# Moving 20 modulation dots from the first feed-forward into both attentions, with a new order of its work and ten wide block pairs

## The chip, the cores and the metric

The kernel runs on one core of a Trainium2 chip. The metric is the device time of one execution in microseconds (us). TensorE (PE in the profile, with PEld for its weight loads) does the matrix products, VectorE (DVE), ScalarE (ACT) and GpSimd (POOL) the elementwise work. SyncE (SP) computes nothing: its queue issues most of the transfers from DRAM, one behind the other, and an issue that has to wait holds up the issues behind it. POOL's queue issues the accumulating transfers.

## The reference

Two layers work on 512 tokens of width 1024. Layer 0 mixes the tokens by stick-breaking attention, layer 1 by an indexer-selected sparse attention (16 heads, a top-k selection, a relative bias). Behind each comes a gated feed-forward of width 2816 with a causal convolution over 3 tokens. All norms and residuals are modulated by six vectors a layer that come from the condition `c`:

```python
cond = silu(c)
for i in range(2):
    mod = cond @ ada_w[i] + ada_b[i]
    sh1, sc1, g1, sh2, sc2, g2 = split(mod, 6)
    h = rms_norm(x, norm_mix[i]) * (1 + sc1) + sh1
    mix = stick_breaking_attention(h, ...) if i == 0 else dsa_attention(h, ...)
    x = x + g1 * mix
    h = rms_norm(x, norm_ffn[i]) * (1 + sc2) + sh2
    x = x + g2 * conv_ffn(h, ...)

def conv_ffn(h, w_up, conv_w, conv_b, w_down):
    u = h @ w_up
    y = conv_b + sum(up[:, j:j + S] * conv_w[j] for j in range(3))   # up: u padded by 2 tokens
    gate, val = split(y, 2)
    return (silu(gate) * val) @ w_down
```

## The kernel before

The transposed activations stand on the partitions by feature, 128 at a time. Every product in full precision is made of three products of a shorter format: high by high, low by high and high by low part. So each weight chunk of 128x1024 (512 KB) is loaded as `raw`, ScalarE copies its high part (`whi`), and the low part (`wlo`) is either a subtraction on VectorE or POOL, or ScalarE's negated copy to which a transfer issued by POOL adds the weight once more from DRAM.

**Modulation dots.** `mod` isn't made by TensorE. `ada_dot` multiplies a loaded chunk of `ada_w` (128x1024) by `cond` on VectorE and sums each row; 48 such dots make one layer's modulation. `DOTS` lists those of layer 1 in order of use: six groups `g` of eight. Some are made early, in attention 0 (`ada_steps` once per head), those of `FFN_DOTS[0]` in the first feed-forward, those of `LATE_DOTS` in the late attention of layer 1, and the last eight in the second feed-forward. In the feed-forwards the chunk is a tile named `ada`, elsewhere a `raw`.

**The feed-forward** is not written out in order. `ffn_plan` lists jobs with their engine, duration, predecessors and rings of buffers; `Plan.order` gives each a latest time, counted back from TensorE's fixed order, and sorts every engine's queue by it. Tables steer it: `LEADS` (how early loads are due), `DOT_SPAN` (over which times the dots are spread), `DOWNS_7` and `ORDER_7` (where TensorE's down products go among the up products), and `DOWN_DMA`, `X_DMA`, `ACT_DMA`, `COMBO_DMA`, `PLAIN_DMA` (which low parts and additions go by ScalarE and an accumulating transfer in place of VectorE). There are 22 blocks `j` of the up weights. From block 7 on `up_7` makes a block by seven products of 256 columns instead of eight, with sums and differences of weights and of activations. Each product is 4 chunks deep. In an unmerged block the weight's high part meets the high and the low activations in two 256-wide matmuls; in a block of `MERGED` one 512-wide matmul does both, the halves land beside each other in the bank, and VectorE adds the second half (`side`, six times a block).

**The late attention** of layer 1 (about 724 to 840 us) goes over 16 heads `h`. One round finishes head h and makes the logits of head n = h+1: for each of four query tiles the products `z` (L1925 to L1927), a masked maximum `nm` on VectorE (L1937), an exponential on ScalarE (L2224), transposes `tr` on TensorE (L2234), copies `pT`. `sums(h)` takes the reciprocal of the row sums (L2336). For every odd head it also sends the reciprocals of a pair of heads through DRAM: `rvd` (L2276) writes them and two `bs` (L2282) read them back spread over partitions, all on SP's queue. `th` are the bias rows of a later head (`load_bias`, L1916). `fill` slips in pieces of the query and output projections; their weights are the other `raw` loads (L613).

Of the kernel before, what the change touches and what calls it, by code (L numbers as in the profile page):

```python
# [19 lines left out]
S = 512  # L20
# [42 lines left out]
DOWNS_7 = [[(7, 1), (8, 1), (9, 2), (10, 2), (11, 2), (12, 1), (13, 1), (14, 2), (15, 1), (16, 2), (17, 1), (18, 1), (19, 2),
            (20, 2), (21, 3)],
           [(6, 2), (7, 1), (8, 1), (9, 1), (10, 1), (11, 2), (12, 1), (13, 2), (14, 1), (15, 1), (16, 1), (17, 2), (18, 2),
            (19, 1), (20, 2), (21, 3)]]
ORDER_7 = [['a1', 'd1', 'a2', 'e', 'd2', 'c1', 'down', 'low', 'c2', 'rest'],
           ['a1', 'd1', 'a2', 'e', 'd2', 'down', 'c1', 'low', 'c2', 'rest']]
WEIGHT_7 = {'a1': 0, 'd2': 0, 'a2': 1, 'd1': 13, 'c1': 13, 'e': 24, 'c2': 24}
TAG_7 = {'a': 'mm', 'b': 'x', 'd': 'tr'}  # L70
BANK_7 = {'a1': 'a', 'e': 'a', 'c1': 'a', 'c2': 'a', 'a2': 'b', 'd1': 'd', 'd2': 'd'}
LATE_CHUNKS = [(2, 3), ()]
A_RING = 10
DOT_SPAN = [(30, 310), (5, 270)]
PLAIN_DMA = [[(4, 0), (4, 1), (6, 0), (6, 1)], [(4, 0), (4, 1), (6, 0)]]
DOWN_DMA = [[7, 10, 13, 17, 21], [3, 4, 6, 7, 10, 12, 13, 15, 17, 20, 22]]
LEADS = [{'plain': 38.0, 'r': 8.0, 'sum': 0.5, 'down': 2.0, 'T': 29.5, 'last': 27.5, 'bias': 2.0},
         {'plain': 72.5, 'r': 9.5, 'sum': 3.5, 'down': 3.5, 'T': 10.0, 'last': 0.5, 'bias': 23.0}]
# [160 lines left out]
def ffn_plan(l):  # L239
# [29 lines left out]
    def accumulate(fn, *args, us, after):  # L269
        return p.add("DMA", us * 1.11, None, after=[p.add("POOL", 0.87, fn, *args, after=after)], lag=4.0)  # L270
# [87 lines left out]
    def up_7(j, downs, before):  # L358
        t = p.t
        got1, r1 = load("load_up", j, 1, key=t - lead["r"])  # L360
        got0, r0 = load("load_up", j, 0, key=t - lead["r"] + 0.01)
        s13 = p.add("DVE", 1.22, "sum13", j, after=[got0, got1])
        raw13 = p.place("raw", s13, t - lead["sum"])
        W = {}
        *W[0], n0 = split_by_dma("hi_up", "neg_up", "add_up", (j, 0), r0, got0, 1.05, 3.0, t)
        hi1 = p.add("ACT", 0.62, "hi_half", j, after=[got1])
        both = p.place("whi", hi1, t + 0.1)
        n1 = p.add("ACT", 0.62, "neg_half", j, after=[hi1])
        W[1] = hi1, accumulate("add_half", j, us=1.5, after=[n1]), both, both
# [12 lines left out]
        def then(name, engine, us, fn, arg, needs, ring=None, side=None):  # L382
            if name in done or not all(n in done for n in needs):
                return
            done[name] = p.add(engine, us, fn, j, arg, after=[done[n] for n in needs])
            if ring and ring[0] not in place:
                place[ring[0]] = p.place(ring[1], done[name])
            if merged:
                done[name + "s"] = p.add("DVE", 0.42, "side", j, *side, after=[done[name]])

        def product(what):
            need = [done[n + s_] for n in {"e": ["g0"], "d2": ["v"], "c1": ["x"], "c2": ["v1"]}.get(what, [])]
            if what in ("d1", "d2", "e", "c1"):
# [12 lines left out]
            then("v", "ACT", 0.38, "copy", "v", ["d1"], ("small", "sqt"), ("v", "d"))  # L406
            then("x", "ACT", 0.38, "copy", "x", ["e", "v"], None, ("x", "a"))
            then("v0", "DVE", 0.42, "val", 0, ["x" + s_, "d2"], ("val", "u"), ("v0", "d"))
            then("v1", "DVE", 0.42, "val", 1, ["v" + s_, "c1", "v0"], None, ("v1", "a"))
            then("g2", "ACT", 0.38, "gate", 2, ["c2"], None, ("h", "a"))  # L410

        def finish():
            product("c2")
            place["small"].users += [done["v1"], done["v0"]]
            place["bank a"].users.append(done["g2" + s_])
            place["bank b"].users.append(done["g1" + s_])
            place["bank d"].users.append(done["v0" + s_])
# [24 lines left out]
        return finish  # L442
# [131 lines left out]
def kernel_body(ctx, tc, xT, wst, cst, smalls, crow, ccol, relb, outT):  # L574
# [36 lines left out]
    def chunk_raw(key, n=D):  # L611
        raw = raws.tile([P, D], F32, name="raw")
        nc.sync.dma_start(raw[:, :n], wst[CH[key], :, :n])  # L613
        return raw
# [337 lines left out]
    def stick_layer(l):  # L952
        with ExitStack() as st:
# [481 lines left out]
            for i in range(HN):  # L1435
# [41 lines left out]
    def ffn_layer(l, first, man):  # L1477
        with ExitStack() as st:
# [45 lines left out]
            class do:  # L1524
# [289 lines left out]
    def dsa_layer(l, first, man):  # L1814
        with ExitStack() as st:
# [306 lines left out]
            with ExitStack() as sa:  # L2122
# [218 lines left out]
                for h in range(HEADS):  # L2341
# [210 lines left out]
```

## Time and profile before

| what | us |
|---|---|
| three runs | 1212.32, 1212.98, 1215.43 |
| median | 1212.98 |
| the profiled execution | 1212.47 |
| its span in the trace | 1210.7 |
| TensorE busy | 1204.2 |
| VectorE busy | 1024.2 |
| ScalarE busy | 800.0 |
| POOL busy | 243.5 |

The stages in the trace: attention 0 from about 60 to 262 us, the first feed-forward from about 280 to 603, layer 1's attention from 605 to 862, the second feed-forward to the end. In the rows, `x12` counts instructions, the figure behind it is time, and a bracket such as `[1.66 <-PE tr L2234]` gives the idle time of the engine before the instruction and what ended it. Busy shares are averages over stages; which engine waits for which is read in the stage.

### The profile page before, as it was taken

The numbers are of one execution on the slowest core, as the hardware profiler recorded it, in microseconds if no ns is written. First come the engines' busy times: TensorE is split into PE (matmuls) and PEld (weight loads), VectorE is DVE, ScalarE is ACT, GpSimd is POOL, SyncE is SP. The second block draws the span as 40 slices with busy tenths as digits, with TensorE's granted clock in tenths as the row PEclk, the third lists the DMA queues.
The fourth block names the chain that finished last, engine by engine and source line by source line (L and its number), as shares of the span: only waits on it lengthen the run. The fifth ranks groups of instructions, "written<-read, shape, count | busy, mean of one in ns | idle before, by whom it ended". The sixth has DMA issues, their size and how long they took to land.

```text
span 1210.7 us, 18277 instructions
## 1 busy us (share of the span) xinstructions
PE 1204.2 (99%) x6532; PEld 1009.1 (83%) x6532; DVE 1024.2 (85%) x1736; ACT 800.0 (66%) x1366; POOL 243.5 (20%) x282
## 2 busy tenths in 40 slices
PE   9999999999999999999999999999999999999998
PEld 6888788788898998998888777777888888888887
DVE  5898888998989988999788995668989898889883
ACT  5588787368666676765657357774786677677660
POOL 0001100001111111211000357784012122112110
PEclk9999999999999999999999999999999999999999
DMA  9778897629789898896520242245499888788662
GB/s 377 249 205 231 224 244 240 209 87 220 192 217 277 230 245 217 225 290 174 183 70 18 70 140 57 84 137 167 137 234 212 225 190 204 182 184 190 155 147 87
DMA packets 79923, 224.89 MB, mean 186 GB/s; under 512 B 16588, under 2 KB 17356, under 8 KB 79832
## 3 DMA queue, kind: packets, MB, share of 16 engines
q1 hardware_dynamic: 59616, 169.16, 42.3%
q0 software_dynamic: 20192, 54.54, 25.5%
q8 instruction: 51, 0.84, 0.3%
q14 instruction: 40, 0.33, 0.1%
q10 hardware_dynamic: 24, 0.02, 0.0%
HBM read 212.62 MB, written 2.16 MB: 177 GB/s over the span
## 4 chain that ended last, share of the span: by engine, by line
PE 98%; DMA 1%; ACT 0%; DVE 0%; issue 0%; SPq 0%
PE pt_d L1741 16%; PE pt_a L1653 8%; PE pt_u L1622 6%; PE pt_a L1649 6%; PE pt_d L1653 4%; PE pt_u L1626 3%; PE pt_d L1649 3%; PE pt_q L694 2%; PE pt_q L696 2%; PE pt_l L694 2%; PE pt_q L695 2%; PE pt_l L695 2%; PE pt_l L696 2%; PE pt_qk L694 2%; PE pt_qk L696 2%; PE pt_qk L695 2%
## 5 line engine op out<-in xcount | busy, mean ns | idle before, releaser
L1741 PE MATMUL pt_d<-actlo,dnhi 128*128 128x512 f32 x288 | 112.8, 392 | 0.0
L1741 PE MATMUL pt_d<-acthi,dnhi 128*128 128x512 f32 x288 | 112.8, 392 | 0.0
L1531 ACT ACTIVATE whi<-raw 128x1024 fp32r<-128x1024 f32 x72 | 75.8, 1054 | 29.6 <-PE pt_a L1653 13.1
L644 ACT ACTIVATE whi<-raw 128x1024 fp32r<-128x1024 f32 x80 | 84.2, 1052 | 3.6 <-issue 1.1
L1622 PE MATMUL pt_u<-hh,whi 128*128 128x512 f32 x320 | 75.8, 389 | 0.0
L1741 PE MATMUL pt_d<-acthi,dnlo 128*128 128x512 f32 x288 | 73.5, 391 | 0.0
L662 POOL DMA_DIRECT2D wlo<-wst x23 | 19.9, 866 | 265.2 <-DVE hh L806 114.1
L1622 PEld LDWEIGHTS pt_u<-hh,whi 128*128 128x128 f32 x320 | 60.0, 188 | 12.6 <-issue 0.2
L1543 POOL DMA_DIRECT2D wlo<-wst x37 | 32.0, 865 | 167.1 <-ACT wlo L1539 91.4
L1741 PEld LDWEIGHTS pt_d<-actlo,dnhi 128*128 128x128 f32 x288 | 54.3, 188 | 10.1
L1741 PEld LDWEIGHTS pt_d<-acthi,dnhi 128*128 128x128 f32 x288 | 54.2, 188 | 10.1
L1741 PEld LDWEIGHTS pt_d<-acthi,dnlo 128*128 128x128 f32 x288 | 53.1, 188 | 10.3
L653 POOL TENSOR_TENSOR wlo<-raw,whi 128x1024 fp32r<-128x1024 f32 x18 | 44.2, 2456 | 85.7 <-PE pt_q L695 45.8
L1649 PE MATMUL pt_a<-hh,whi 128*128 128x512 f32 x228 | 61.3, 391 | 0.0
L1349 DVE TENSOR_TENSOR_SCAN mz<-mz,diag 128x768 f32<-128x768 f32 (+1 forms) x32 | 47.6, 1487 | 15.2 <-ACT mz L1343 15.0
L722 DVE SCALAR_TENSOR_TENSOR raw<-raw,cond 128x1024 f32<-128x1024 f32 x46 | 57.3, 1273 | 1.4 <-ACT cond L1167 1.3
L1653 PE MATMUL pt_a<-hh,wlo 128*128 128x256 f32 x360 | 57.4, 282 | 0.0
L1653 PEld LDWEIGHTS pt_a<-hh,wlo 128*128 128x128 f32 x360 | 53.1, 190 | 4.5
L1937 DVE CUSTOM_DVE_ANT_0 L<-z,L,cols 128x128 f32<-128x128 f32 (+3 forms) x60 | 32.3, 546 | 28.7 <-PE tr L2234 20.7
L1554 POOL DMA_DIRECT2D whi<-wst x30 | 26.0, 866 | 132.8 <-ACT whi L1551 82.6
L694 PE MATMUL pt_q<-hh,whi 128*128 128x512 f32 x128 | 51.8, 405 | 0.0
L722 DVE SCALAR_TENSOR_TENSOR ada<-ada,cond 128x1024 f32<-128x1024 f32 x41 | 50.0, 1219 | 1.7 <-DMA ada<-wst 1.7
(409 smaller groups left out, 3803.3 us busy)
## 6 DMA issues: line engine op xcount, KB each, us to landing
raw<-wst SPq DMA_DIRECT2D x215, 512.0 KB, 5.2
wlo<-wst POOLq DMA_DIRECT2D x60, 512.0 KB, 7.8
ada<-wst SPq DMA_DIRECT2D x45, 512.0 KB, 5.4
raw<-wst SPq DMA_DIRECT2D x48, 384.0 KB, 4.8
whi<-wst POOLq DMA_DIRECT2D x30, 256.0 KB, 5.8
dnlo<-wst POOLq DMA_DIRECT2D x16, 384.0 KB, 7.0
x<-xt POOLq DMA_DIRECT2D x18, 256.0 KB, 5.6
th<-relb SPq DMA_DIRECT2D x16, 256.0 KB, 4.0
```

What stands on the lines that cost most here:

```text
L644: act.activation(hi[:, :n], raw[:, :n], AF.Copy)
L653: engine.tensor_sub(lo[:, :w], raw[:, :w], hi[:, :w].bitcast(F32))
L694: pe.matmul(out, lhsT=whi, rhs=ahi, start=start, stop=False)
L695: pe.matmul(out, lhsT=wlo, rhs=ahi, start=False, stop=False)
L696: pe.matmul(out, lhsT=whi, rhs=alo, start=False, stop=stop)
L722: dve.scalar_tensor_tensor(raw, raw, 1.0, cond, op0=OP.mult, op1=OP.mult, accum_out=dst)
L1349: dve.tensor_tensor_scan(rev, rev, diag[:, b:e][:, ::-1], 0.0, OP.mult, OP.max)
L1531: act.activation(W[j, i][0], R[j, i], AF.Copy)
L1622: pe.matmul(pt[j, i], lhsT=W[j, i][0][:, k * P:(k + 1) * P], rhs=hs[k][n], start=k + n == 0, stop=False)
L1649: pe.matmul(pt[j, bank, "both"], lhsT=w[:, c0 + k * P:c0 + (k + 1) * P], rhs=a[2], start=new and k == 0, stop=False, skip_group_check=True)
L1653: pe.matmul(out, lhsT=w[:, c0 + k * P:c0 + (k + 1) * P], rhs=a[n], start=new and k + n == 0, stop=part == 1 and k == 3 and what in ("a2", ...
L1741: pe.matmul(pt["dn", i], lhsT=dn[i][part][:, k * P:(k + 1) * P], rhs=A[j0 + k][n], start=part + k + n == 0, stop=part == 1 and k == j1 - j ...
```

## The change

Of layer 1's dots, 11 instead of 4 are made early in attention 0, 13 instead of 33 in the first feed-forward, and 16 instead of 3 in the late attention, where now each head has one dot behind its reciprocal and each round one load. In the first feed-forward 10 blocks instead of 5 are merged, and the tables move low parts between the engines: for 12 blocks the up weight's low part and for 6 the half weight's go from ScalarE and a transfer to VectorE, and 11 low parts of down weights, 5 additions to `x` and 4 low parts of activations go from VectorE to ScalarE and a transfer. The due times are set anew. The second feed-forward's tables stay as they were.

```diff
-ORDER_7 = [['a1', 'd1', 'a2', 'e', 'd2', 'c1', 'down', 'low', 'c2', 'rest'],
+ORDER_7 = [['a1', 'd1', 'a2', 'e', 'd2', 'c1', 'down', 'c2', 'low', 'rest'], ...
-DOT_SPAN = [(30, 310), (5, 270)]
+DOT_SPAN = [(145, 405), (5, 270)]
-DOWN_DMA = [[7, 10, 13, 17, 21], [3, 4, 6, 7, 10, 12, 13, 15, 17, 20, 22]]
+DOWN_DMA = [[0, 1, 2, 4, 5, 7, 9, 10, 12, 13, 15, 16, 17, 18, 19, 21], [3, 4, 6, 7, 10, 12, 13, 15, 17, 20, 22]]
-MERGED = [[10, 15, 16, 20, 21], [7, 9, 10, 11, 12, 13, 14, 15, 16, 17, 18, 19, 20, 21]]
+MERGED = [[8, 9, 11, 13, 14, 15, 16, 19, 20, 21], [7, 9, 10, 11, 12, 13, 14, 15, 16, 17, 18, 19, 20, 21]]
-X_DMA = [[1, 2, 8, 10, 11, 13, 19, 20, 22, 23], [1, 2, 6, 9, 13, 20, 22, 23]]
-ACT_DMA = [[2, 5, 9, 15], [4, 7, 8, 9, 13, 15, 20]]
+X_DMA = [[0, 2, 5, 6, 9, 10, 12, 14, 15, 16, 18, 19, 20, 21, 23], [1, 2, 6, 9, 13, 20, 22, 23]]
+ACT_DMA = [[3, 4, 5, 6, 7, 12, 14, 19], [4, 7, 8, 9, 13, 15, 20]]
+W0_DVE = [[7, 8, 9, 10, 12, 13, 15, 17, 18, 19, 20, 21], []]
+W1_DVE = [[7, 9, 10, 14, 20, 21], []]
 DOTS = [(1, g, f) for g in range(6) for f in range(8)]
-LATE_DOTS = DOTS[37:40]
-FFN_DOTS = [DOTS[4:37], DOTS[40:]]
+EARLY_DOTS = 11
+LATE_DOTS = DOTS[24:40]
+FFN_DOTS = [DOTS[EARLY_DOTS:24], DOTS[40:]]
...
-        *W[0], n0 = split_by_dma("hi_up", "neg_up", "add_up", (j, 0), r0, got0, 1.05, 3.0, t)
+        if j in W0_DVE[l]:
+            W[0] = split("hi_up", "lo_up", (j, 0), r0, got0, 1.05, 1.22, t)
+            n0 = W[0][1]
+        else:
+            *W[0], n0 = split_by_dma("hi_up", "neg_up", "add_up", (j, 0), r0, got0, 1.05, 3.0, t)
...
+        if j in W1_DVE[l]:
+            n1 = p.add("DVE", 0.69, "lo_half", j, after=[hi1])
+            W[1] = hi1, n1, both, both
+        else:
...
-    ada_jobs = [(0, g, f) for g in (2, 3, 4, 5) for f in range(KT)] + DOTS[:4]
+    ada_jobs = [(0, g, f) for g in (2, 3, 4, 5) for f in range(KT)] + DOTS[:EARLY_DOTS]
...
-                ada_steps(3 if i % 4 == 3 else 2)
+                ada_steps(2 if i % 3 == 2 else 3)
...
+                def lo_half(j):
+                    put((j, 1), 1, W[j, 1][0])
+                    dve.tensor_sub(W[j, 1][1][:, S:], R[j, 1][:, S:], W[j, 1][0][:, :S].bitcast(F32))
...
-                raw_dots = []
+                raw_dots, dots_left = [], list(LATE_DOTS)

                 def load_dots(n):
-                    raw_dots.extend((d, chunk_raw(("ada",) + d)) for d in LATE_DOTS[len(raw_dots):][:n])
+                    for _ in range(min(n, len(dots_left))):
+                        d = dots_left.pop(0)
+                        raw_dots.append((d, chunk_raw(("ada",) + d)))
...
                 load_bias(3)
+                load_dots(1)
...
                     follow(dve)
                     if h == 3:
                         q_newton(8, EARLY_Q)
-                    if h == HEADS - 2:
-                        late_dots(2)
-                    if not more:
-                        late_dots(1)
+                    late_dots(1)
...
                         for j in range(2, QT):
                             masked_bias(h + 2, j)
+                    load_dots(1)
                     if n + 3 < HEADS:
                         load_bias(n + 3)
...
                     if h == HEADS - 4:
-                        load_dots(3)
                         bias_job(2, "col")
```

Three places in the order of instructions. First, TensorE in block 8 of the first feed-forward, which is newly merged: `pt_a`, `pt_d` and `pt_b` are the banks, `hh` activations, `tt` their combinations. Before:

```order
L1653 MATMUL pt_a<-hh,whi 128x256 x8
L1653 MATMUL pt_a<-hh,wlo 128x256 x4
L1653 MATMUL pt_d<-tt,whi 128x256 x8
L1653 MATMUL pt_d<-tt,wlo 128x256 x4
L1653 MATMUL pt_b<-hh,whi 128x256 x12
```

After:

```order
L1663 MATMUL pt_a<-hh,whi 128x512 x4
L1667 MATMUL pt_a<-hh,wlo 128x256 x4
L1663 MATMUL pt_d<-tt,whi 128x512 x4
L1667 MATMUL pt_d<-tt,wlo 128x256 x4
L1663 MATMUL pt_b<-hh,whi 128x512 x4
L1667 MATMUL pt_b<-hh,whi 128x256 x4
```

Eight narrow matmuls have become four wide ones in each product. Lines are those of the changed kernel, where the wide product stands at L1663 and the narrow one at L1667.

Second, SP's queue in the late attention from the `rvd` of heads 6 and 7 to that of heads 8 and 9; numbers are those of buffers. Before:

```order
L2276 DMA rvd_7951<-rv_7762 128x2x4
L2282 DMA bs_7971<-rvd_7951 64x512 x2
L1916 DMA th_8000<-relb 128x512
L1916 DMA th_8084<-relb 128x512
L613 DMA raw_8094<-wst 128x1024
L2276 DMA rvd_8130<-rv_7928 128x2x4
```

After:

```order
L2292 DMA rvd_7836<-rv_7641 128x2x4
L2298 DMA bs_7858<-rvd_7836 64x512 x2
L623 DMA raw_7887<-wst 128x1024
L1930 DMA th_7889<-relb 128x512
L623 DMA raw_7974<-wst 128x1024
L1930 DMA th_7976<-relb 128x512
L623 DMA raw_7986<-wst 128x1024
L2292 DMA rvd_8022<-rv_7813 128x2x4
```

The load `raw_7887` of head 8's dot stands behind the two `bs` of head 7, `raw_7974` of head 9's behind the next `th`.

Third, VectorE at head 8, from its reciprocal `rv` to the maximum of the next head's fourth tile. Before:

```order
L2336 RECIPROCAL rv_7928<-sum_7930 128x4
L1937 ISA L2_7994,nm_8015<-z_8053,L2_7994,cols_6316 128x384
L1937 ISA nm_8015 128x1
L2241 COPY pT_8041<-tr_8059 128x512
L1937 ISA L3_7997,nm_8015<-z_8068,L3_7997,cols_6316 128x512
```

After:

```order
L2353 RECIPROCAL rv_7813<-sum_7815 128x4
L732 SCALAR_TENSOR_TENSOR raw_7887,mod1_88<-raw_7887,cond_86 128x1024
L1951 ISA L2_7881,nm_7904<-z_7943,L2_7881,cols_6178 128x384
L1951 ISA nm_7904 128x1
L2257 COPY pT_7930<-tr_7949 128x512
L1951 ISA L3_7884,nm_7904<-z_7958,L3_7884,cols_6178 128x512
```

The dot of `raw_7887` now stands between the reciprocal and the maximum.

More of the change, by code (lines that the diff above doesn't have):

```diff
@@ L62 @@
 FIRST_7 = [7, 7]
[L63 to L66, printed above, removed]
-ORDER_7 = [['a1', 'd1', 'a2', 'e', 'd2', 'c1', 'down', 'low', 'c2', 'rest'],
-           ['a1', 'd1', 'a2', 'e', 'd2', 'down', 'c1', 'low', 'c2', 'rest']]
+DOWNS_7 = [[(7, 2), (8, 1), (9, 2), (10, 1), (11, 2), (12, 2), (13, 2), (14, 1), (15, 1), (16, 1), (17, 1), (18, 2),
+           (19, 1), (20, 2), (21, 3)], [(6, 2), (7, 1), (8, 1), (9, 1), (10, 1), (11, 2), (12, 1), (13, 2), (14, 1),
+           (15, 1), (16, 1), (17, 2), (18, 2), (19, 1), (20, 2), (21, 3)]]
+ORDER_7 = [['a1', 'd1', 'a2', 'e', 'd2', 'c1', 'down', 'c2', 'low', 'rest'], ['a1', 'd1', 'a2', 'e', 'd2', 'down',
+           'c1', 'low', 'c2', 'rest']]
 WEIGHT_7 = {'a1': 0, 'd2': 0, 'a2': 1, 'd1': 13, 'c1': 13, 'e': 24, 'c2': 24}
@@ L73 @@
 A_RING = 10
-DOT_SPAN = [(30, 310), (5, 270)]
-PLAIN_DMA = [[(4, 0), (4, 1), (6, 0), (6, 1)], [(4, 0), (4, 1), (6, 0)]]
-DOWN_DMA = [[7, 10, 13, 17, 21], [3, 4, 6, 7, 10, 12, 13, 15, 17, 20, 22]]
-LEADS = [{'plain': 38.0, 'r': 8.0, 'sum': 0.5, 'down': 2.0, 'T': 29.5, 'last': 27.5, 'bias': 2.0},
-         {'plain': 72.5, 'r': 9.5, 'sum': 3.5, 'down': 3.5, 'T': 10.0, 'last': 0.5, 'bias': 23.0}]
-FFN_BIAS = [(1, 4), (1, 10)]
-MERGED = [[10, 15, 16, 20, 21], [7, 9, 10, 11, 12, 13, 14, 15, 16, 17, 18, 19, 20, 21]]
-X_DMA = [[1, 2, 8, 10, 11, 13, 19, 20, 22, 23], [1, 2, 6, 9, 13, 20, 22, 23]]
-ACT_DMA = [[2, 5, 9, 15], [4, 7, 8, 9, 13, 15, 20]]
+DOT_SPAN = [(145, 405), (5, 270)]
+PLAIN_DMA = [[(4, 0), (5, 0), (5, 1), (6, 1)], [(4, 0), (4, 1), (6, 0)]]
+DOWN_DMA = [[0, 1, 2, 4, 5, 7, 9, 10, 12, 13, 15, 16, 17, 18, 19, 21], [3, 4, 6, 7, 10, 12, 13, 15, 17, 20, 22]]
+LEADS = [{'plain': 81.5, 'r': 17.0, 'sum': 10.5, 'down': 19.5, 'T': 32.0, 'last': 1.0, 'bias': 131.0}, {'plain': 72.5,
+         'r': 9.5, 'sum': 3.5, 'down': 3.5, 'T': 10.0, 'last': 0.5, 'bias': 23.0}]
+FFN_BIAS = [(1, 0), (1, 6)]
+MERGED = [[8, 9, 11, 13, 14, 15, 16, 19, 20, 21], [7, 9, 10, 11, 12, 13, 14, 15, 16, 17, 18, 19, 20, 21]]
+X_DMA = [[0, 2, 5, 6, 9, 10, 12, 14, 15, 16, 18, 19, 20, 21, 23], [1, 2, 6, 9, 13, 20, 22, 23]]
+ACT_DMA = [[3, 4, 5, 6, 7, 12, 14, 19], [4, 7, 8, 9, 13, 15, 20]]
 XT = 2
-COMBO_DMA = [[(2, 0)], [(1, 0), (1, 1), (3, 0), (3, 1)]]
+W0_DVE = [[7, 8, 9, 10, 12, 13, 15, 17, 18, 19, 20, 21], []]
+W1_DVE = [[7, 9, 10, 14, 20, 21], []]
+COMBO_DMA = [[(2, 1)], [(1, 0), (1, 1), (3, 0), (3, 1)]]
 DOTS = [(1, g, f) for g in range(6) for f in range(8)]
-LATE_DOTS = DOTS[37:40]
-FFN_DOTS = [DOTS[4:37], DOTS[40:]]
+EARLY_DOTS = 11
+LATE_DOTS = DOTS[24:40]
+FFN_DOTS = [DOTS[EARLY_DOTS:24], DOTS[40:]]
 class Job:
@@ L364, in up_7 @@
         W = {}
-        *W[0], n0 = split_by_dma("hi_up", "neg_up", "add_up", (j, 0), r0, got0, 1.05, 3.0, t)
+        if j in W0_DVE[l]:
[3 more added lines that the diff above has]
+            *W[0], n0 = split_by_dma("hi_up", "neg_up", "add_up", (j, 0), r0, got0, 1.05, 3.0, t)
         hi1 = p.add("ACT", 0.62, "hi_half", j, after=[got1])
         both = p.place("whi", hi1, t + 0.1)
-        n1 = p.add("ACT", 0.62, "neg_half", j, after=[hi1])
-        W[1] = hi1, accumulate("add_half", j, us=1.5, after=[n1]), both, both
+        if j in W1_DVE[l]:
+            n1 = p.add("DVE", 0.69, "lo_half", j, after=[hi1])
+            W[1] = hi1, n1, both, both
+        else:
+            n1 = p.add("ACT", 0.62, "neg_half", j, after=[hi1])
+            W[1] = hi1, accumulate("add_half", j, us=1.5, after=[n1]), both, both
         r1.users += [hi1, n1]
```

## Prediction

> **What bounds the kernel now.** I read the page first, then busy time by stage, then the critical chain inside the first feed-forward, then single engines around the three places that the change edits. The page's head, its row of busy times and its chain:
>
> ```profile
> span 1210.7 us, 18277 instructions
> ...
> PE 1204.2 (99%) x6532; PEld 1009.1 (83%) x6532; DVE 1024.2 (85%) x1736; ACT 800.0 (66%) x1366; POOL 243.5 (20%) x282
> ...
> PE 98%; DMA 1%; ACT 0%; DVE 0%; issue 0%; SPq 0%
> ```
>
> TensorE is busy in 1204.2 of 1210.7 us and the chain that ends last is 98% TensorE. So time can only fall if matmuls are removed or made shorter, or if some of the 1210.7 - 1204.2 = 6.5 us without a matmul vanish; it rises when another engine's wait reaches TensorE. The stages that the change edits are attention 0 (60 to 240 us), the first feed-forward (290 to 600) and the late attention of layer 1 (724 to 830):
>
> ```profile
> core 0: us, PE busy (x) PEld busy (x) DVE busy (x) ACT busy (x) POOL busy (x), PEclk, DMA share, GB/s
> 60.00:240.00 180.00, 179.95 (x1036) 145.51 (x1036) 157.20 (x199) 133.21 (x267) 12.93 (x15) 1.00 0.78 224
> 290.00:600.00 310.00, 310.00 (x1826) 275.89 (x1825) 278.30 (x434) 204.20 (x308) 46.78 (x54) 1.00 0.84 226
> 724.00:830.00 106.00, 104.81 (x653) 83.36 (x652) 69.97 (x200) 76.59 (x197) 82.61 (x92) 1.00 0.35 101
> ```
>
> In the feed-forward TensorE never idles, so taking dots off VectorE there relieves nothing that TensorE waits for: the gain is not in the moved dots but at most in what else changes in TensorE's own work. VectorE looks free in the late attention (69.97 of 106 us), but that is an average; what counts is where its idle stretches lie and when a dot's data arrive.
>
> **Merging, the one edit that shortens TensorE's work.** Five more blocks (5 to 10) feed a weight's high part through one 512-wide matmul in place of two 256-wide ones. One product, unmerged and merged, in the critical chain (start, us, what):
>
> ```profile
> 335.18 1.44 PE pt_d L1653 x12
> ...
> 381.77 0.93 PE pt_d L1649 x4
> 382.70 0.47 PE pt_d L1653 x4
> ```
>
> Twelve narrow matmuls take 1.44; four wide and four narrow take 0.93 + 0.47 = 1.40. That is 0.04 us a product, with 7 products in each of 5 blocks: 35 x 0.04 = 1.4 us saved, on the path. The figures are rounded to 0.01 each, so 0.03 to 0.05, or 1.0 to 1.8 us.
>
> **VectorE and the rest in the first feed-forward.** VectorE's groups there (line, engine, operation, shapes, count | busy, mean ns | idle before):
>
> ```profile
> L722 DVE SCALAR_TENSOR_TENSOR ada<-ada,cond 128x1024 f32<-128x1024 f32 x33 | 40.2, 1220 | 1.4 <-DMA ada<-wst 1.4
> L1535 DVE TENSOR_TENSOR wlo<-raw,whi 128x1024 fp32r<-128x1024 f32 x17 | 20.8, 1224 | 5.1 <-ACT whi L1531 4.9
> ...
> L1725 DVE TENSOR_TENSOR dnlo<-raw,dnhi 128x768 fp32r<-128x768 f32 x19 | 18.1, 954 | 1.8 <-ACT dnhi L1722 1.8
> ...
> L1708 DVE TENSOR_TENSOR actlo<-y,acthi 128x512 fp32r<-128x512 f32 x16 | 11.0, 686 | 0.8 <-ACT acthi L1705 0.7
> L816 DVE SCALAR_TENSOR_TENSOR x<-pt_d,mod,x 128x512 f32<-128x512 f32 x14 | 10.5, 748 | 1.5 <-PE pt_d L1741 1.5
> L1566 DVE TENSOR_TENSOR raw<-raw 128x512 f32<-128x512 f32 x15 | 10.3, 688 | 0.2
> ...
> L1689 DVE TENSOR_TENSOR gate<-gate,pt_a 128x256 f32<-128x256 f32 x10 | 4.1, 417 | 0.4 <-ACT gate L1675 0.3
> ```
>
> Away: 20 dots x 1.220 = 24.4; 11 low parts of the down weights x 0.954 = 10.5; 5 additions to x x 0.748 = 3.7; 4 low parts of the activations x 0.686 = 2.7. Added: 5 blocks x 6 side additions x 0.417 = 12.5; 12 low parts of up weights x 1.224 = 14.7 (before, ScalarE and a POOL-issued transfer made them); 6 half-width low parts, of the size of L1566, x 0.688 = 4.1. Net -24.4 - 10.5 - 3.7 - 2.7 + 12.5 + 14.7 + 4.1 = -10.0 us of the 278.3. ScalarE loses 18 negations and gains 20 smaller passes, and with 204.2 of 310 us busy has room. The DMA loses 20 loads of 512 KB, 12 accumulating transfers of 512 KB and 6 of 256 KB, and gains 11 of 384 KB and 9 of 256 KB, under a share of 0.84. I take 0: VectorE, still about 268 of 310 us, and the lighter DMA queues are the cover. Were that cover gone, a late low part would hold TensorE for up to its own length, 1.22 us, and I leave 0 to +2 us for one or two such places among the reshuffled due times. The swap of the low down product and the last product c2 only trades two pieces of TensorE work.
>
> **Attention 0.** Seven more dots, 7 x 1.22 = 8.5 us, in VectorE's idle time of 180 - 157.2 = 22.8 us. Tightest is the last head, where the multiply that makes `a` precedes the transposes on TensorE:
>
> ```profile
> 227.41 0.69 DVE L1350 TENSOR_TENSOR a<-a,mz 128x511 f32<-128x511 f32 x1
> ...
> 229.40 0.60 PE L1366 MATMUL tr<-cons,a 128*128 128x128 f32 x4
> ```
>
> 229.40 - 228.10 = 1.3 us of slack. Steps 12 and 13 take one dot more each, 2.44 us, of which the idle time ahead of this multiply absorbs part; what passes on must exceed 1.3 us to be felt. I take 0, with 0 to +1.
>
> **The late attention: 13 more dots, one behind every reciprocal.** Here the place on two queues decides. On SP the load of the dot for an even head h+1 now stands behind `rvd` and the two `bs` of the odd head h, and `bs` reads what `rvd` wrote to DRAM. On VectorE the dot stands directly behind the head's reciprocal, ahead of the masked max of that head's third tile (L1937, 128x384), which feeds the exponentials and the transposes. Before, the three loads went out at head 12 for dots at heads 14 and 15. SP's rows (start, length) and the transfer time of a 512 KB raw load in this stretch:
>
> ```profile
> 734.91 1.15 SPq L2282 DMA_DIRECT2D bs<-rvd  x2
> 764.41 1.09 SPq L2282 DMA_DIRECT2D bs<-rvd  x2
> 775.19 0.91 SPq L2276 DMA_DIRECT2D rvd<-rv  x1
> 778.92 1.09 SPq L2282 DMA_DIRECT2D bs<-rvd  x2
> 793.71 1.83 SPq L2282 DMA_DIRECT2D bs<-rvd  x2
> 808.70 1.09 SPq L2282 DMA_DIRECT2D bs<-rvd  x2
> ...
> L613 SPq DMA_DIRECT2D raw<-wst x15: 327/426/1239, 753.7 to 844.1; - x15
> ...
> DMA to landing us min/median/max: 3.6/4.9/5.9
> ```
>
> SP's queue stands still from 776.10 (775.19 + 0.91) to 778.92 for that round trip. A load issued at the end of the `bs` pair lands 4.9 us later and its dot ends 1.22 after that, 6.12 us in all. The maxes that would follow:
>
> ```profile
> 741.37 0.62 DVE L1937 CUSTOM_DVE_ANT_0 L<-z,L,cols 128x384 f32<-128x384 f32 x1 [4.23 <-PE tr L2234]
> 770.84 0.62 DVE L1937 CUSTOM_DVE_ANT_0 L<-z,L,cols 128x384 f32<-128x384 f32 x1 [3.60 <-PE tr L2234]
> 783.82 0.62 DVE L1937 CUSTOM_DVE_ANT_0 L<-z,L,cols 128x384 f32<-128x384 f32 x1 [1.66 <-PE tr L2234]
> 798.44 0.62 DVE L1937 CUSTOM_DVE_ANT_0 L<-z,L,cols 128x384 f32<-128x384 f32 x1 [0.30 <-PE tr L2234]
> 812.73 0.62 DVE L1937 CUSTOM_DVE_ANT_0 L<-z,L,cols 128x384 f32<-128x384 f32 x1 [1.37 <-PE tr L2234]
> ```
>
> Lateness of the max: head 2, 736.06 + 6.12 - 741.37 = 0.8; head 6, 765.50 + 6.12 - 770.84 = 0.8; head 8, 780.01 + 6.12 - 783.82 = 2.3; head 10, 795.54 + 6.12 - 798.44 = 3.2; head 12, 809.79 + 6.12 - 812.73 = 3.2. What of it TensorE feels depends on the slack of its next consumers:
>
> ```profile
> 785.75 0.72 ACT L2224 ACTIVATE L<-L,nm 128x512 f32<-128x512 f32 x1 [0.57 <-DVE nm L1937]
> 787.45 0.60 PE L2234 MATMUL tr<-cons,L 128*128 128x128 f32 x4
> ...
> 801.05 0.39 PE L1925 MATMUL z<-kph,qh 128*128 128x256 f32 x1 [0.42 <-DVE nm L1937]
> ...
> 814.66 0.72 ACT L2224 ACTIVATE L<-L,nm 128x512 f32<-128x512 f32 x1 [0.57 <-DVE nm L1937]
> 815.85 0.60 PE L2234 MATMUL tr<-cons,L 128*128 128x128 f32 x4
> ```
>
> Near head 8 the exponential ends at 786.47, 0.98 ahead of the transposes: 2.3 - 0.98 = 1.3 us of stall. Near head 10 TensorE already waits 0.42 for VectorE, so all 3.2 are felt. Near head 12 the exponential ends at 815.38, 0.47 ahead: 3.2 - 0.47 = 2.7. Heads 2 and 6 lie between nothing and all of 0.8; I take half each, 0.8 together. The dots of odd heads are loaded a whole head before their use, with no `rvd` between: 0, at most 1.5 together if their 1.22 us meet a busy VectorE. Sum 1.3 + 3.2 + 2.7 + 0.8 = 8.0 us. With the shortest landing, 3.6, each lateness falls by 1.3 and 0 + 1.9 + 1.4 = 3.3 is left; with the longest, 5.9, it is 2.3 + 4.2 + 3.7 + 2 x 1.8 = 13.8, and 15.3 with the odd heads. I take the median, since these are the same loads in the same stretch.
>
> **The sum.** The profiled execution took 1212.47 us, its span 1210.7 and 1.8 around it, and is 0.5 below the median of the runs. 1212.47 - 1.4 + 0 + 0 + 8.0 = 1219.1 us; with the bounds of the late attention 1214.4 to 1226.4.
>
> **Rivals.** (B) The dots cost nothing there, and only the merging shows: 1212.47 - 1.4 = 1211.1 us, not slower. For it: VectorE idles 1.66 to 4.23 us ahead of several of these maxes, so data that came in time would fit. It decides if a load lands within some 2.5 us of its issue, or if it can leave ahead of the `bs` pair; against it, the shortest landing is 3.6 and the order has it behind. (C) A lock between VectorE and POOL adds to the stalls. The two late dots that ran back to back before:
>
> ```profile
> L722 DVE SCALAR_TENSOR_TENSOR raw<-raw,cond 128x1024 f32<-128x1024 f32 x2 | 4.8, 2440 | 0.0
> ...
> 825.37 3.40 DVE L722 SCALAR_TENSOR_TENSOR raw<-raw,cond 128x1024 f32<-128x1024 f32 x1
> ```
>
> They took 2440 ns on the mean against 1220 elsewhere, and POOL is busy 82.61 of 106 us here with 92 operations, 0.90 us each. A dot that comes at a random moment then waits 0.78 x 0.45 = 0.35 us, 13 x 0.35 = 4.6 in all: 1219.1 + 4.6 = 1223.7. At the rate of those two dots it would be 13 x 1.22 = 15.9; against that, they ran beside a whole weight subtraction on POOL, which most heads don't place there. The Trainium skill ("SBUF — State Buffer", section "Who interferes with whom") says that a VectorE instruction with two SBUF inputs contends with a GpSimd instruction that reads SBUF, and that whoever is first keeps the shared pair for the whole instruction. The 2440 ns agree with it; by that rule the waits would also run the other way, POOL behind a dot. (D) The reordered feed-forward, or the last heads of attention 0, stalls TensorE by its upper ends (+2 and +1) and more, with the late attention free: 1211.1 + 3 = 1214.1 and up; TensorE's 310.00 of 310.00 busy before speaks against it. (E) Faster: the merging's 1.8 and over 2 of the 6.5 us without a matmul vanish together; 1208.8 or less. Nothing in the edits removes a wait that the rows show.
>
> **How the numbers follow.** A measurement of this kernel tells about 0.3%, 3.6 us, from no change. Chances: the forecast 0.60 (0.04 of it within 3.6 us, at the shortest landings), B 0.27, C 0.06, D 0.04 (slower than 0.3%), E 0.03. So slower 0.56 + 0.06 + 0.04 = 0.66, the same 0.27 + 0.04 = 0.31, faster 0.03. The time is that of the forecast, 1219.1, its own range 1214.4 to 1226.4. As B and the forecast differ in sign and hold 0.87, the range reaches from B at the larger saving, 1212.47 - 1.8 = 1210.7, rounded to 1210.5, to the upper end 1226.4.
>
> **What would show it.** Merged products of 1.40 us in blocks 8, 9, 11, 13, 14, 19 of the first feed-forward, and TensorE without a gap there: merging and the rest right. In the late attention, dots of heads 8, 10 and 12 that idle 2 to 4 us for a load of the raw tile, and behind them TensorE waiting 1 to 3 us for VectorE or ScalarE: the forecast right. Dots that start without a wait, or loads issued ahead of the `bs` pair, make it wrong (B). Dots of 2 us and more beside POOL show C; TensorE gaps in 60 to 600 us show D. The prediction fails if the stalls total under 3 us, or if a POOL delay spreads to every head.

## The result and the profile after

The changed kernel takes 1229.42 us (median of 5 runs, 1226.94 to 1231.26) against 1212.96: a ratio of 1.013, 95% interval 1.0118 to 1.0142. It is 16.5 us slower, where 6.1 was forecast. The profiled execution took 1231.26 us. The head of its page, its busy times and its chain:

```profile
span 1229.5 us, 18024 instructions
...
PE 1210.8 (98%) x6392; PEld 1005.3 (82%) x6392; DVE 1046.0 (85%) x1769; ACT 798.4 (65%) x1368; POOL 254.7 (21%) x284
...
PE 87%; DVE 6%; DMA 3%; issue 1%; ACT 1%; POOL 1%; SPq 0%; DVEq 0%; ACTq 0%
```

TensorE was busy 6.6 us longer although 140 instructions fewer ran on it, and its idle time rose from 6.5 to 18.7 us. The chain, all but pure TensorE before, now goes through VectorE and transfers for 9% of the span. By stage, layer 1 from the late attention to the second feed-forward, before and after (columns as before: length, then busy time and count of each engine, the granted clock, the DMA's share and rate):

```profile
717.00:885.00 168.00, 166.81 (x950) 133.11 (x945) 127.14 (x294) 113.74 (x255) 93.61 (x102) 1.00 0.41 120
```

```profile
717.00:903.00 186.00, 173.32 (x941) 137.40 (x941) 147.44 (x318) 113.54 (x254) 102.95 (x101) 0.96 0.49 145
```

The two windows hold the same work of TensorE to within 1 us. It took 18 us longer: TensorE's idle time is 12.7 instead of 1.2 us, and its busy time 6.5 us more, at a mean granted clock of 0.96. What TensorE waited for between 717 and 850 us, before and after (waiter, line, who ended the wait: total, times, longest):

```profile
PE av L2265 <- ACT vals L2252: 0.7, 1, 0.7
PE z L1925 <- DVE nm L1937: 0.4, 1, 0.4
```

```profile
PE z L1939 <- DVE nm L1951: 6.3, 8, 2.7
PE pt_o L704 <- DVE x L826: 3.7, 1, 3.7
PE av L2281 <- ACT vals L2268: 2.5, 4, 0.7
...
DVE raw L732 <- DMA raw<-wst: 14.1, 8, 4.4
```

The last row is VectorE's own: eight dots stood 14.1 us in front of a raw tile that hadn't landed, and TensorE waited 10 us behind VectorE. The two longest of these waits, at heads 0 and 10, on SP's queue, on VectorE and on TensorE:

```profile
720.67 2.48 SPq L1930 DMA_DIRECT2D th<-relb  x1
723.24 0.86 SPq L623 DMA_DIRECT2D raw<-wst  x2
...
729.23 1.23 DVE L732 SCALAR_TENSOR_TENSOR raw<-raw,cond 128x1024 f32<-128x1024 f32 x1 [4.36 <-DMA raw<-wst]
...
731.05 0.33 PE L1939 MATMUL z<-kph,qh 128*128 128x128 f32 x1 [2.68 <-DVE nm L1951]
...
732.32 0.58 PE L1939 MATMUL z<-kph,qh 128*128 128x256 f32 x1 [0.72 <-DVE nm L1951]
```

```profile
799.93 0.43 SPq L2292 DMA_DIRECT2D rvd<-rv  x1
805.54 1.87 SPq L2298 DMA_DIRECT2D bs<-rvd  x2
807.51 0.53 SPq L623 DMA_DIRECT2D raw<-wst  x1
...
812.16 1.23 DVE L732 SCALAR_TENSOR_TENSOR raw<-raw,cond 128x1024 f32<-128x1024 f32 x1 [2.37 <-DMA raw<-wst]
...
814.11 0.79 PE L704 MATMUL pt_o<-ohi,whi 128*128 128x512 f32 x1 [3.69 <-DVE x L826]
```

Head 0's load stood behind a `th` that waited on the queue until 723.15, head 10's behind `rvd` and the `bs` pair. The matmul at 814.11 took 0.79 us; one of that size took 0.50 behind the wait of 0.45 us at 223 us. Windows ahead of, in and behind the two slow stretches show why:

```profile
728.00:731.00 3.00, 0.38 (x2) 0.00 (x0) 1.77 (x5) 0.00 (x0) 0.10 (x1) 1.00 0.28 115
731.00:738.00 7.00, 6.23 (x22) 5.41 (x23) 4.53 (x13) 4.96 (x13) 3.66 (x4) 0.54 0.13 38
738.00:745.00 7.00, 7.00 (x47) 5.16 (x46) 4.03 (x12) 4.88 (x12) 4.55 (x5) 0.97 0.55 138
806.00:810.00 4.00, 4.00 (x28) 3.19 (x25) 2.57 (x8) 1.58 (x6) 2.96 (x4) 1.00 0.44 123
810.00:814.00 4.00, 0.41 (x3) 0.14 (x1) 1.84 (x4) 0.03 (x1) 3.61 (x4) 0.93 0.84 277
814.00:820.00 6.00, 5.61 (x18) 4.75 (x19) 5.96 (x16) 4.16 (x9) 2.05 (x2) 0.50 0.05 17
```

Behind each long wait the granted clock stood at 0.5 for about 7 us, and TensorE did in that time about half its work. That is where its 6.6 us of extra busy time are, and it is a cost that the forecast did not have.

### The profile page after: what moved, and what is told of

Read it like the earlier page. It is cut to its first block, busy times and chain, and to the rows that moved or that the text cites. A ratio compares the mean times of both kernels' runs of the same rounds, so it can differ in the third digit from the quotient of the medians.

```text
span 1229.5 us, 18024 instructions
## 1 busy us (share of the span) xinstructions
PE 1210.8 (98%) x6392; PEld 1005.3 (82%) x6392; DVE 1046.0 (85%) x1769; ACT 798.4 (65%) x1368; POOL 254.7 (21%) x284
## 4 chain that ended last, share of the span: by engine, by line
PE 87%; DVE 6%; DMA 3%; issue 1%; ACT 1%; POOL 1%; SPq 0%; DVEq 0%; ACTq 0%
PE pt_d L1755 16%; PE pt_a L1663 7%; PE pt_a L1667 6%; PE pt_u L1636 6%; PE pt_d L1663 4%; PE pt_d L1667 3%; PE pt_u L1640 3%; PE pt_l L704 2%; PE pt_l L705 2%; PE pt_l L706 2%; DMA raw<-wst 2%; PE pt_qk L704 2%; PE pt_qk L706 2%; PE pt_qk L705 2%; PE pt_fv L1109 2%; PE pt_b L1663 2%
## 5 line engine op out<-in xcount | busy, mean ns | idle before, releaser
L732 DVE SCALAR_TENSOR_TENSOR raw<-raw,cond 128x1024 f32<-128x1024 f32 x66 | 85.7, 1325 | 15.4 <-DMA raw<-wst 14.1
L1663 PE MATMUL pt_a<-hh,whi 128*128 128x512 f32 x288 | 77.4, 390 | 0.0
L672 POOL DMA_DIRECT2D wlo<-wst x23 | 19.9, 865 | 265.9 <-ACT wlo L671 89.3
L1545 DVE TENSOR_TENSOR wlo<-raw,whi 128x1024 fp32r<-128x1024 f32 x47 | 57.3, 1220 | 4.6 <-ACT whi L1541 3.8
L1663 PEld LDWEIGHTS pt_a<-hh,whi 128*128 128x128 f32 x288 | 52.9, 188 | 10.1
L2221 POOL TENSOR_TENSOR L<-L,maskb 128x128 f32<-128x128 f32 (+3 forms) x60 | 54.8, 927 | 28.5 <-ACT L L2220 25.2
L2240 ACT ACTIVATE L<-L,nm 128x128 f32<-128x128 f32 (+3 forms) x60 | 33.5, 558 | 40.8 <-DVE nm L1951 40.8
L1667 PEld LDWEIGHTS pt_a<-hh,wlo 128*128 128x128 f32 x360 | 54.0, 189 | 5.7
L1667 PE MATMUL pt_a<-hh,wlo 128*128 128x256 f32 x360 | 57.3, 281 | 0.0
L1746 POOL DMA_DIRECT2D dnlo<-wst x27 | 23.5, 872 | 149.6 <-ACT dnlo L1742 96.1
```

What stands on the lines that cost most here:

```text
L732: dve.scalar_tensor_tensor(raw, raw, 1.0, cond, op0=OP.mult, op1=OP.mult, accum_out=dst)
L1545: dve.tensor_sub(W[j, i][1], R[j, i], W[j, i][0].bitcast(F32))
L1663: pe.matmul(pt[j, bank, "both"], lhsT=w[:, c0 + k * P:c0 + (k + 1) * P], rhs=a[2], start=new and k == 0, stop=False, skip_group_check=True)
L1667: pe.matmul(out, lhsT=w[:, c0 + k * P:c0 + (k + 1) * P], rhs=a[n], start=new and k + n == 0, stop=part == 1 and k == 3 and what in ("a2", ...
L2221: pool.tensor_add(L, L, maskb[:, LOFF[j]:LOFF[j] + ns])
```

## The experiments

**The loads, one head earlier.** The theory was that the dots' data come late and that the long wait then halves the clock; the rival was that the dots' own work and its contention with POOL are the cost.

```diff
+                load_dots(1)
                 load_bias(2)
                 begin(0)
...
                 load_bias(3)
                 load_dots(1)
```

> The changed kernel with one more dot load ahead of the late attention: every late dot's load goes out one head earlier (the first one ahead of the bias rows), the dots stay where they are on VectorE. Theory A (the dots are late because their loads stand behind th, rvd and bs on SP's queue, and a long enough TensorE gap then halves the granted clock): VectorE no longer idles for a raw tile ahead of a dot, no TensorE gap over 1 us between 724 and 840 us, granted clock 1.00 throughout, 1211 to 1215 us. Theory B (the 13 dots' own VectorE time and the contention with POOL are the cost): it stays within 3 us of the changed kernel, 1226 to 1231 us.

1221.39 us (1.0063 of before, 1.005 to 1.0077). No dot waited for a tile any more, and both long waits were gone: 8.0 of the 16.5 us came from the late loads and the clock behind them. But 8.4 us stayed, outside both ranges given: each theory holds for half. TensorE's waits between 717 and 850 us:

```profile
PE z L1939 <- DVE nm L1951: 3.6, 6, 1.2
PE av L2281 <- ACT vals L2268: 3.3, 6, 0.7
PE pt_o L704 <- DVE x L826: 0.6, 1, 0.6
```

**No loads at all.** The late dots read `cond` twice.

```diff
-                        raw_dots.append((d, chunk_raw(("ada",) + d)))
+                        raw_dots.append((d, raws.tile([P, D], F32, name="raw")))
...
-                        ada_dot(mod[l][:, g * KT + f:g * KT + f + 1], raw)
+                        dve.scalar_tensor_tensor(raw, cond, 1.0, cond, ..., accum_out=mod[l][:, g * KT + f:g * KT + f + 1])
```

> The changed kernel with the 16 late dots computed from resident data: no load is issued for them (so these 16 columns of the modulation come from other data), each dot stays where it is on VectorE with the same size and two inputs. Theory A: no wait for a transfer is left, so no gap of 2.5 us; what is left is the dots' own VectorE time and the contention with POOL, as in the run with the loads ahead: 1219 to 1223 us. Theory E (the 13 further transfers slow the other loads of the late attention, and that is what the loads-ahead run still paid): 1215 us or less.

1220.89 us (1.0066, 1.0052 to 1.008), as theory A says. It takes 0.5 us less than with the loads ahead, inside both intervals. So the transfers as such cost nothing that can be seen here; only their lateness did.

**One input in place of two.** This is to part the contention from the dots' own time. The edit also takes away the dot's output of 128x1024 and its `raw` tile.

```diff
-                        ada_dot(mod[l][:, g * KT + f:g * KT + f + 1], raw)
+                        dve.tensor_reduce(out=mod[l][:, g * KT + f:g * KT + f + 1], in_=cond, op=OP.add, axis=AX.X)
```

> As the run without loads, but each of the 16 late dots is a reduction of one resident 128x1024 tile (one input in place of two, no big output; the columns of the modulation come from other data). VectorE works about as long, nothing is loaded. If the contention with POOL is most of what was left (1220.9 us without loads): reductions at one even length, olo back near 0.7 us, POOL's additions back near 0.8 us, 1213 to 1216 us. If the dots' own time on VectorE is most of it: 1218 us or more.

1215.5 us (1.0023, 1.0014 to 1.0032), in the range of contention. The late dots, and POOL's additions, by groups from 724 to 840 us (count | busy, mean ns of one | idle before), first without loads and then with one input:

```profile
L2205 DVE SCALAR_TENSOR_TENSOR raw<-cond 128x1024 f32<-128x1024 f32 x15 | 22.5, 1503 | 0.0
...
L2222 POOL TENSOR_TENSOR L<-L,maskb 128x512 f32<-128x512 f32 (+3 forms) x57 | 52.5, 934 | 17.5 <-ACT L L2221 14.7 <-DVE L L2217 0.4
```

```profile
L2205 DVE TENSOR_REDUCE mod<-cond 128x1 f32<-128x1024 f32 x16 | 19.1, 1192 | 0.0
...
L2221 POOL TENSOR_TENSOR L<-L,maskb 128x512 f32<-128x512 f32 (+3 forms) x57 | 45.7, 814 | 22.7 <-ACT L L2220 20.0 <-DVE L L2216 0.4
```

With one input an operation takes an even 1192 ns (the longest 1210), and POOL's additions 814 ns, nearly as before the change (807 in the same window). With two inputs both are longer, 1503 and 934. `olo`, itself an operation with two inputs, stayed at 0.94 us (0.86 in this window before), so that part of the expectation was wrong. By the medians the difference is 1220.89 - 1215.5 = 5.4 us, but not all of it is contention. The two profiled executions, both at a mean clock of 0.998, lie 1220.35 - 1216.87 = 3.5 us apart, and TensorE's waits between 717 and 850 us fall from 6.8 to 3.5 us. Only three of the ten runs with one input are at that clock (median 1216.74), the four runs without loads all at 0.998 or 0.999. So at equal clock it is 3.5 to 4.1 us; the rest goes with a short slow stretch that most runs with one input don't have. What the missing output and the 16 free `raw` tiles add to the difference, no run here parts. The Trainium skill ("SBUF — State Buffer", "Who interferes with whom") has the rule, that two SBUF inputs on VectorE contend with a GpSimd instruction that reads SBUF, while a reduction doesn't; both halves of it agree with these means.

**The late dots alone**, on the kernel before (the table and the late attention's lines of the diff, `LATE_DOTS = DOTS[24:40]`, `FFN_DOTS = [DOTS[4:24], DOTS[40:]]`).

> The kernel before with only the late dots of the change: 16 instead of 3 in the late attention, with the change's loads and places, 20 instead of 33 in the first feed-forward; everything else as before. Theory A: the whole loss is here, without the merging's gain: 1228 to 1233 us, with TensorE gaps of 2.5 us and more at heads 0 and 10 and a granted clock of 0.5 behind them. Theory C (attention 0 or the new order of the feed-forward carries a part of at least 3 us): 1225 us or less.

1233.84 us (1.017, 1.0157 to 1.0184), with TensorE waits of 2.41 and 3.12 us at heads 0 and 10 and two stretches at half clock. That is 0.8 above the range of theory A and far from theory C's, so this part carries the loss. It is 4.4 us slower than the whole change: 2.5 are delays in the first feed-forward, where 20 dots run under the tables for 33, and it lacks the merging.

**Only the first load ahead**, before `load_bias(2)` instead of behind `load_bias(3)`.

> The changed kernel with only head 0's load moved ahead of the two bias rows; the other loads as in the change. Theory A: the gap of 2.7 us at head 0 goes (2.85 + 0.88 us in the changed kernel) and with it its stretch of half clock (some 3.3 us), 6 to 7 us in all, and the gap at head 10 with its slow stretch stays: 1222 to 1224 us. If the later heads take up the slack (the head 0 stall only delayed what would wait anyway): 1227 us or more.

1225.28 us (1.0102, 1.0087 to 1.0118), missed by 1.3 us. The wait and the slow stretch at head 0 were gone, those at head 10 (3.39 us, and 7 us at half clock) stayed. Between the profiled executions, of which that of the change had both, the difference is 1231.26 - 1225.33 = 5.9 us, near the 6 to 7 expected; between the medians it is only 4.1. The runs of the change spread from 1226.94 us at a mean clock of 0.997 to 1231.26 at 0.994, so the time at half clock differs between its runs. Behind it head 3's wait grew from 0.57 to 1.09 us.

**Waits of known cause.** Spare multiplications on VectorE, in the kernel before, with nothing loaded.

```diff
+                    for _ in range({8: 3, 10: 2, 6: 5, 12: 4, 2: 7}.get(h, 0)):
+                        spin = raws.tile([P, D], F32, name="raw")
+                        dve.tensor_mul(spin, cond, cond)
```

> The kernel before with extra VectorE multiplications of resident data (128x1024, nothing loaded, results unused) behind the reciprocals of heads 2, 6, 8, 10 and 12: 7, 5, 3, 2 and 4 of them. By the idle times and slacks of before they make TensorE gaps of about 3.8, 2.5, 1.0, 2.1 and 3.0 us. Theory A (the gap itself halves the clock): the granted clock falls to 0.5 for about 7 us behind the gaps of 3 us and more, perhaps behind 2.5, never behind 1.0; 12.4 us of gaps and 3.3 us for each slow stretch, 1228 to 1235 us. Theory D (the low clock has another cause, such as the transfers in flight): clock 1.00 throughout, 1225 us.

1235.79 us in one run, 0.8 above theory A's range. The multiplications took 1622 ns each on the mean. The waits at heads 2 and 6 came out longer than expected and those behind them shorter: 5.33, 4.65, 0.58 (behind ScalarE), 1.40 and 2.17 us in order of time. Windows at and behind that of head 2, and behind those of heads 10 and 12:

```profile
743.00:748.00 5.00, 1.14 (x5) 0.57 (x4) 5.00 (x5) 0.00 (x0) 4.92 (x3) 1.00 0.00 0
748.00:755.00 7.00, 5.17 (x17) 4.43 (x18) 5.59 (x16) 4.99 (x13) 4.12 (x6) 0.51 0.13 35
755.00:760.00 5.00, 5.00 (x35) 4.45 (x35) 4.00 (x13) 3.62 (x10) 2.18 (x4) 1.00 0.20 59
...
821.00:826.00 5.00, 5.00 (x34) 4.44 (x34) 3.83 (x12) 5.00 (x12) 3.71 (x3) 1.00 0.33 81
...
839.00:844.00 5.00, 5.00 (x34) 4.40 (x33) 4.23 (x13) 4.34 (x13) 3.96 (x5) 1.00 0.03 1
```

The clock fell to 0.5 for 7 us behind the waits of 5.33 and 4.65 us (0.51 and 0.54 on the mean of 7 us), and during both no transfer was in flight (DMA share 0.00); it stayed at 1.00 behind 2.17 and 1.40. So the wait itself does it. The limit is no single length: in the changed kernel 2.68 us, followed by three small matmuls and 0.72 more, was enough. Short waits do it at times only. With the loads ahead, 0.53, 0.72 and 0.71 us in a row at head 3 brought 3.4 us at half clock, and 0.62 and 1.20 at head 10 none. Without loads it was the other way round: nothing behind 0.52, 0.72 and 0.70, and 3.4 us behind 0.62 and 1.21. What differs is where the waits lie in time. In each trace here the granted clock changes only at whole steps of 3.41 us from the trace's other changes; the full speed between the two slow stretches of the changed kernel, for one, lasts 75.09 us, 22 such steps. Single steps, first with the loads ahead, then without loads:

```profile
750.04:753.45 3.41, 1.83 (x9) 1.01 (x7) 3.41 (x10) 1.68 (x5) 0.00 (x0) 1.00 0.84 225
753.45:756.86 3.41, 3.03 (x8) 1.00 (x10) 1.81 (x7) 2.78 (x6) 2.50 (x2) 0.50 0.21 56
```

```profile
749.43:752.84 3.41, 2.17 (x11) 1.42 (x11) 3.41 (x9) 1.00 (x4) 0.22 (x1) 1.00 0.44 79
804.05:807.46 3.41, 1.59 (x9) 1.08 (x7) 3.41 (x10) 0.71 (x3) 2.70 (x4) 1.00 0.00 0
807.46:810.87 3.41, 3.39 (x12) 3.01 (x13) 3.40 (x9) 3.41 (x7) 2.02 (x2) 0.50 0.08 28
```

Of the same three waits the step with the loads ahead took in 1.58 us (TensorE busy 1.83 of 3.41), the step without loads only 1.24 (2.17 busy). Over all traces here, ahead of their last few us, the clock fell behind every step in which TensorE was busy for up to 1.59 us and behind none with 1.95 or more; between the two it fell behind 1.83 and 1.92 (loads ahead, one input) and stayed behind 1.67, 1.78 (the multiplications) and 1.92 (only the first load ahead). So the limit lies near half a step, and these busy times, whose ends are modelled, show it no closer. The full clock came back behind steps with 3.03 us and more and not behind 2.80 and less, so a stretch lasted one step or two, and longer where the wait itself did.

The Trainium skill ("TensorE: Matmul & The Clock Gate", "Part 1: The HAM clock gate (the "warmup" mystery)") tells of a free-running window of about 3.4 us, of half the clock after at least one idle window, and of the full clock after a busy one. The steps of 3.41 us agree with that window; but a window didn't have to be idle here, since 1.92 us of work in one did not keep the clock up.

**The merging alone** (only `MERGED`).

> The kernel before with only the ten merged blocks of the change in the first feed-forward (30 more side additions, same dots and tables). By the rows of before 35 products x 0.04 us: 1.0 to 1.8 us faster, 1211.2 to 1212.0 us. If VectorE, 12.5 us fuller there with 33 dots in place, turns into the bound: slower than before by 2 us or more, with TensorE gaps behind VectorE between 290 and 600 us.

1214.32 us (1.0009, 1.0 to 1.0018), between the two expectations: no gain. TensorE waited, for the first time in this stage, behind VectorE's side additions:

```profile
405.80 0.98 PE L1649 MATMUL pt_a<-hh,whi 128*128 128x512 f32 x3 [0.63 <-DVE vx L1689]
```

By the starts of the matmuls, delays in this stage cost 2.6 us together (0.1 before), more than the 1.4 saved, with VectorE busy 290.76 of 313 us.

**Merging with the early dots**: the ten merged blocks, and 11 dots in attention 0, 26 in the first feed-forward.

> The kernel before with the ten merged blocks and 11 dots early in attention 0 (26 in the first feed-forward), all other tables as before, late dots as before. The merging alone left 2.1 us of gaps in the feed-forward with 33 dots there; with 7 dots fewer (8.5 us of VectorE time) they should shrink: 1211.5 to 1213.5 us. If attention 0 doesn't bear the 7 dots: a gap over 0.5 us near 222 us, where the changed kernel shows 0.6, and no gain.

1213.79 us (1.0007, 0.9998 to 1.0016), 0.3 above the range: not told apart from before. The delays in the feed-forward shrank to 1.7 us, and attention 0 paid with one of 0.45 us.

**The change without its late dots**, 26 dots in the first feed-forward.

> The changed kernel with the late dots as before (3), the 13 others back in the first feed-forward (26 there), the rest of the change kept. If the feed-forward's new plan bears them: TensorE without a gap there, 1.4 us of merging gained, 1211 to 1212 us. If the merging needs the dots away, as the run with the merging alone suggests: gaps of 2 us and more behind VectorE between 290 and 600 us, 1213 us or more.

1249.35 us (1.0301, 1.0287 to 1.0315), through a single wait at the end of the feed-forward:

```profile
626.38 0.80 PE L704 MATMUL pt_l<-acthi,whi 128*128 128x512 f32 x1 [33.91 <-ACT whi L654]
```

> The changed kernel with 3 late dots and 26 in the first feed-forward, as in the run that stalled 34 us at the end of the feed-forward, but with the dots' due times of before (30 to 310 in place of 145 to 405). If the late due times caused that stall: no gap at the end, 1211 to 1213 us, the merging's gain kept. If VectorE can't bear 26 dots under the new plan: gaps behind VectorE inside the feed-forward, 1215 us or more.

With the dots' old due times (30 to 310) that wait was gone, but another of 10.51 us stood at 334 us, where the first block of seven products starts: 1225.39 us (1.0103, 1.0089 to 1.0117). Tables made for 13 dots don't carry 26 under either span.

**The dots where VectorE idled**, loads two heads ahead.

```diff
+                late_at = {2: 3, 3: 1, 4: 3, 5: 1, 6: 2, 7: 1, 8: 1, 9: 1, 11: 1, 12: 1, 14: 1}
...
+                    late_dots(late_at.get(h, 0))
                     follow(dve)
...
-                    load_dots(1)
+                    load_dots(late_at.get(h + 2, 0))
```

> The changed kernel with its 16 late dots placed by VectorE's idle times of before: 3, 1, 3, 1, 2, 1, 1, 1 at heads 2 to 9 and one each at 11, 12 and 14, ahead of the events that follow the reciprocal, none at heads 0, 1, 10, 13 and 15; every load two heads ahead. Theory A with the places as the second cause: no gap over 1 us, clock 1.00, 1211 to 1214 us. If the dots' contention with POOL is what is left wherever they stand: 1217 us or more.

1219.38 us (1.0054, 1.0041 to 1.0066): 2 us better than the loads ahead alone, clock at 1.00, still 6.8 slower than before. The idle time of before was not free: POOL works in it.

```profile
L732 DVE SCALAR_TENSOR_TENSOR raw<-raw,cond 128x1024 f32<-128x1024 f32 x16 | 27.3, 1727 | 0.0
...
738.40 3.41 DVE L732 SCALAR_TENSOR_TENSOR raw<-raw,cond 128x1024 f32<-128x1024 f32 x1
```

The dots took 1727 ns on the mean, one of them 3.41 us, and TensorE waited 1.22 us at 761 us for a weight subtraction on POOL, where the first theory expected none over 1 us. That fits the second theory, 1217 us or more. No version here beats the kernel before.

## Why the prediction was right or wrong

The direction, the place and the first link were right: the late attention, loads behind `rvd` and `bs`, dots that wait for a raw tile, TensorE behind VectorE. The time was outside the range. Point by point:

- **Merging, 1.4 us: right in the change, not on its own.** Between the first product of the seven and the start of the late attention (334 to 717 us) the changed kernel gained 1.2 us, with no wait in the feed-forward. But the sentence that taking dots off VectorE relieves nothing was too short: under the tables and dots of before the merging gains nothing (1214.32 us). How much of the room came from the dots and how much from the moved low parts no run here parts. The cover that I named for the rest held.
- **Attention 0, 0 to +1: 0.5 us**, one wait for `x` at 223 us, not at the transposes of 229 us that I had called tightest.
- **The late attention, 8.0 us: the step that failed.** It measured about 19 us in the profiled execution. Its terms were these:
  - Head 10 was right in kind and size: 3.2 forecast, 3.69 measured, `rvd` and `bs` as named.
  - Head 0 was missing. I looked for `rvd` ahead of the loads and not for `th`, which waits on the same queue for its buffer; 2.68 and 0.72 us.
  - Heads 8 and 12 were too high: 1.3 and 2.7 forecast; TensorE didn't wait for head 8's dot, and 0.6 us for head 12's. Nor did it wait behind those of heads 2 and 6 (0.8 together), though they idled 1.12 and 2.13 us for their tiles. The lateness was worked out on the times of before, with the rounds of the odd heads unchanged. For head 8 one sees what that missed: TensorE's waits of 0.55 and 0.71 us in head 7's round stood between the `bs` pair and head 8's dot, gave the load that time, and the dot idled only 0.32 us. That the longer odd rounds did the same for the others is argued, not shown.
  - The odd heads themselves, 0 to 1.5 forecast, held waits of 0.2 to 0.7 us at heads 3, 5 and 7, 4.2 us together, of which 0.7 stood there before. Head 3 has a chain of small column operations on VectorE ahead of its dot, so there is no idle time for it.
  - The clock behind a long wait, about 3.5 us each time, was in no term and no rival.
- **Rival C was no rival but a part of the sum.** It was priced at 4.6 us and given 0.06; the runs put it at 3.5 to 4.1 us at equal clock and 5.4 between medians, on top of the rest. The two stretched dots of before had shown it. That most heads place no weight subtraction there did not excuse it: POOL's additions, 57 of them, were longer beside the dots too (934 ns against 814).
- Rival B fell with the first row of waits, and D with a feed-forward free of gaps.

Put together from medians, before at 1212.7: -1.4 for the merging; +8.5 for late loads and half clock (1229.4 - 1220.9); +5.4 for the contention, with the short slow stretches that go with it; and 4.2 as what is left (1215.5 - 1212.7 + 1.4), which I put down to the dots' own time at heads without room and to attention 0, and which no run parts further. That is 1229.4; the terms are differences between runs and add up by construction, so the sum proves none of them.

## What to carry to other kernels

Work that moves into an engine's idle time needs three things at its new place, and each is read in another view: its data in time (everything that waits on the queue ahead of its load, not only the transfer), idle time in that very round, and no neighbour that makes both engines' operations longer. When waits leave TensorE busy for less than about half of some 3.4 us, count with the slow clock behind them: here 3.4 us lost for 7 us at half speed. And a lateness that is worked out on the old times is safe for the first head only, since every delay moves what stands behind it: four of the five estimates here (heads 2, 6, 8 and 12) came out too high.

## What the runs showed of the hardware

Single waits of 2.41 us (the late dots alone) to 5.33 us on TensorE were followed by about 7 us at a granted clock of 0.5, the longest with no transfer in flight; 2.17 us were not. In every trace the granted clock changed at whole steps of 3.41 us from its other changes. It fell behind every step with up to 1.59 us of work on TensorE and behind none with 1.95 or more, so that 0.53, 0.72 and 0.71 us in a row brought 3.4 us of half clock in one kernel and the same three none in another. An operation of 128x1024 with two inputs took 1220 ns in the first feed-forward, where POOL was busy 46.78 of 310 us, and 1503 to 1727 ns on the mean in the late attention beside POOL; a reduction of one input of that size took 1192 ns there, and POOL's additions 814 ns instead of 934.
